# A trunk of attention, dense and expert layers: the first expert chosen on the chip, narrower first slot, whole weight chunks

## The chip, the cores and the metric

The kernel runs on one core of a Trainium2 chip, as one launch. The metric is the device time of an execution in microseconds (us). The engines of a core are TensorE (PE), VectorE (DVE), ScalarE (ACT), GpSimd (POOL) and SyncE (SP), each with its own instruction stream; they wait for each other by semaphores. DMAs are issued from SP, ACT and GpSimd queues.

## What is computed

512 tokens of width 1024 pass two post-norm layers. Layer 0 is sliding-window attention with cross-attention and a dense SwiGLU; layer 1 is forgetting attention with cross-attention and a top-2-of-8 mixture of experts. The part that matters here is the mixture (F is 2816):

```python
logits = (x2 @ w_router).astype(jnp.float32) + b_router.astype(jnp.float32)
top_vals, top_idx = lax.top_k(logits, TOP_K)
gates = jax.nn.softmax(top_vals, axis=-1)
...
def expert_block(args):
    xb, e = args
    h = xb @ w_in[e]
    return (jax.nn.silu(h[:, :D_FF]) * h[:, D_FF:]) @ w_out[e]
...
y = jnp.zeros_like(x2).at[slot_tok].add((ys * slot_gate[:, None]).astype(x2.dtype))
```

Each token goes to its two best experts, and a layer norm of 1.414 x + y follows. For the reference's inputs the experts 0 to 7 get 111, 128, 98, 133, 134, 128, 135 and 157 tokens; of the first 384 tokens 83, 95, 78, 108, 95, 95, 105 and 109.

## The kernel before

All weights are float32 and are read once, in chunks of 128 x 2048 (1 MiB). `Weights` (from L78) handles them: `load` issues a chunk's DMA on SP into a ring of raw buffers (7 in the expert part), `upper` writes the float16 high half `wh` on ACT (L149), and `lower` the float16 rest `wl` on DVE (L158), both in pieces of `PIECE` = 1048 columns (1048 and 1000). A ring of `NHL` = 7 chunks holds the halves. Each float32 product is three matmuls: wh by the high half of the activations, wh by their low half, wl by the high half (L1442 to L1444 and L1471 to L1473). `need` forces what a matmul needs; else the splitting advances by `tick`, which is called from within the products and issues one high piece and, one piece later, its low half. `tick` is called four times in a unit. Tile's scheduler keeps the order of each engine as the program is written, so where a `tick` stands sets what lies ahead of an instruction on ACT and DVE.

The expert part has eight slots, in a fixed order of work; slot s has `CAP[s]` places, that is columns of the activations, and the loops over it are unrolled. A table `TURN` says which rank by count sits in which slot, except that expert 0 is always in slot 0. Its token rows are gathered by matmuls with one-hots (`choose`, `oh_`), while the other slots' rows come by indirect DMA from the rows in HBM (`fetch`, `ready`). For slots 1 to 7 the expert's number is computed on DVE and read by SP (`value_load`, L296), and the chunk addresses come from it. Slot 0 has a fixed address, so its first chunks load ahead, during attention.

A slot has 22 input chunks (ten units of 512 columns in `block4`, two chunks and 96 matmuls each, and a `gate_pair`) and 11 output chunks (`down_wide`), 1584 matmuls in all; the last slot (`down_direct`) has 12 of them. Units come in pairs: even ones are the gate, odd ones the up half. A unit's products go to one of two PSUM banks (`bank2`). The gate's bank is read by ACT, the up half's by DVE (`quad`, L1458, tile `sa`: gate times up), after which ACT makes the high half of the product and GpSimd subtracts it (L1460). So unit i + 2 cannot start before unit i's bank is read, and for odd units that is an instruction in DVE's stream, behind all `wl` that stand ahead of it.

Between the units jobs are hung (`at`): in slot 6 the sums of the earlier slots come back from HBM (`token_sums`, unit 5), are normed (`stats`, units 7 and 8; `norm_out`, units 10 to 13), and the rows of slots 6 and 7 are joined to them in slot 7 (`rows_out`, `rows_done`). At the start, DVE also makes the list of slots (`order_of`, `lists`), the gates and their parts (`gates`, `gate_parts`), and one-hots (`places`).

## Time and profile before

| | us |
| --- | --- |
| median of 3 runs | 1633.73 |
| lowest to highest | 1633.63 to 1635.57 |
| the profiled execution | 1634.23 |
| its span, first to last instruction | 1632.4 |
| PE busy in the span | 1578.6 |
| DVE busy | 1210.9 |
| ACT busy | 950.3 |
| GpSimd busy | 267.7 |

The span holds attention and the dense layer up to about 789 us; the eight slots follow to 1620.5 us, and 12 us of last norms and stores. The profile's windows give the busy time of each engine in a stretch, and the granted clock of PE (1.00 is 2.4 GHz, 0.5 is 1.2 GHz). The timelines give each instruction's start and duration, and in brackets the idle time of its engine before it with what ended it.

### The profile page before, as it was taken

To read this page: it belongs to the slowest core of one execution; us is meant where nothing else is said; L and a number is where in the kernel's file an instruction comes from. 1 tells how busy PE (TensorE), PEld (TensorE's weight loads), DVE (VectorE), ACT (ScalarE), POOL (GpSimd) and SP (SyncE) were. 2 spreads that over 40 slices of the span, in tenths; PEclk is the share of its full clock that TensorE was granted. 3 is DMA by queue.
4 is the path that set the end of the run, shared out by engine and by line. 5 is a ranking of instruction groups with operands and counts; after the bars stand their busy time and mean duration, and the time that the engine had idled before them with its cause. 6 is when DMAs were issued, how large, how long until landed. Compare 5 with 4: busy or idle time off the path is not lost. (4 is left out here: it accounts for less than half of the span.)

```text
span 1632.4 us, 42978 instructions
## 1 busy us (share of the span) xinstructions
PE 1578.6 (97%) x18640; PEld 1267.8 (78%) x18640; DVE 1210.9 (74%) x1811; ACT 950.3 (58%) x1447; POOL 267.7 (16%) x264
## 2 busy tenths in 40 slices
...
GB/s 275 178 53 53 27 129 104 103 104 91 219 114 60 53 129 92 66 27 65 308 363 364 293 394 377 352 370 305 390 357 361 375 320 373 329 297 360 358 369 113
DMA packets 180549, 370.16 MB, mean 227 GB/s; under 512 B 6589, under 2 KB 49597, under 8 KB 180352
## 3 DMA queue, kind: packets, MB, share of 16 engines
...
q14 instruction: 49, 0.40, 0.1%
...
## 5 line engine op out<-in xcount | busy, mean ns | idle before, releaser
L158 DVE SCALAR_TENSOR_TENSOR wl<-raw,wh 128x1048 f16<-128x1048 f32 (+3 forms) x658 | 794.7, 1258 | 100.3 <-ACT wh L149 100.1
L149 ACT ACTIVATE wh<-raw 128x1048 f16<-128x1048 f32 (+3 forms) x658 | 641.8, 1036 | 101.7 <-PE bk L239 42.9
L1444 PE MATMUL bk<-xa,wl 128*128 128x160 f16 (+3 forms) x1280 | 260.0, 231 | 0.9 <-DVE wl L158 0.9
L1442 PE MATMUL bk<-xa,wh 128*128 128x160 f16 (+3 forms) x1280 | 260.1, 231 | 0.8 <-ACT xa L231 0.8
L1443 PE MATMUL bk<-xa,wh 128*128 128x160 f16 (+3 forms) x1280 | 260.0, 231 | 0.0
L1443 PEld LDWEIGHTS <-wh 128*128 128x128 f16 x2560 | 250.5, 98 | 3.6 <-issue 2.4
L1444 PEld LDWEIGHTS <-wl 128*128 128x128 f16 x2560 | 250.5, 98 | 1.3 <-DVE wl L158 1.1
L1442 PEld LDWEIGHTS <-wh 128*128 128x128 f16 x2560 | 250.4, 98 | 0.7
L1473 PE MATMUL bk<-act,wl 128*128 128x160 f16 (+6 forms) x1232 | 235.3, 227 | 1.2 <-DVE wl L158 1.2
L1472 PE MATMUL bk<-act,wh 128*128 128x160 f16 (+6 forms) x1232 | 235.3, 227 | 0.0
L1471 PE MATMUL bk<-act,wh 128*128 128x160 f16 (+6 forms) x1232 | 235.2, 227 | 0.0
L1442 PE MATMUL bk<-xe,wh 128*128 128x128 f16 (+2 forms) x1280 | 223.2, 221 | 2.2 <-DVE sa L1458 1.4
L1443 PE MATMUL bk<-xe,wh 128*128 128x128 f16 (+2 forms) x1280 | 223.1, 221 | 0.0
L1444 PE MATMUL bk<-xe,wl 128*128 128x128 f16 (+2 forms) x1280 | 223.1, 221 | 0.0
L237 PE MATMUL bk<-xTh,wh 128*128 128x512 f16 (+2 forms) x656 | 204.8, 322 | 1.2 <-DVE Kx L234 0.9
L239 PE MATMUL bk<-xTh,wl 128*128 128x512 f16 (+2 forms) x656 | 204.6, 322 | 1.4 <-DVE wl L158 1.4
L238 PE MATMUL bk<-xTl,wh 128*128 128x512 f16 (+2 forms) x656 | 204.6, 322 | 0.5 <-DVE xTl L234 0.5
L1460 POOL TENSOR_TENSOR act<-sa,act 128x512 f16<-128x512 f32 (+6 forms) x40 | 106.3, 2659 | 284.7 <-ACT act L231 284.6
L239 PEld LDWEIGHTS <-wl 128*128 128x128 f16 x944 | 92.4, 98 | 49.0 <-DVE wl L158 2.9
L237 PEld LDWEIGHTS <-wh 128*128 128x128 f16 x944 | 92.4, 98 | 48.7 <-ACT wh L149 2.0
L238 PEld LDWEIGHTS <-wh 128*128 128x128 f16 x944 | 92.5, 98 | 46.6 <-issue 1.5
L1473 PEld LDWEIGHTS <-wl 128*128 128x128 f16 x1232 | 120.5, 98 | 1.6 <-DVE wl L158 1.6
(349 smaller groups left out, 2669.2 us busy)
## 6 DMA issues: line engine op xcount, KB each, us to landing
...
```

The source lines that it names most:

```text
L149: self.nc.scalar.activation(h[:, p:e], t[:, p:e], AF.Copy, scale=SW)
L158: self.nc.vector.scalar_tensor_tensor(l, src, SW, h, op0=OP.mult, op1=OP.subtract)
L237: nc.tensor.matmul(o, lh, rh, start=first, stop=False, **kw)
L238: nc.tensor.matmul(o, lh, rl, start=False, stop=False, **kw)
L239: nc.tensor.matmul(o, ll, rh, start=False, stop=last, **kw)
L1442: nc.tensor.matmul(o, wh[:, k, c], xe[0][:, k, :C], start=first, stop=False, skip_group_check=True)
L1443: nc.tensor.matmul(o, wh[:, k, c], xe[1][:, k, :C], start=False, stop=False, skip_group_check=True)
L1444: nc.tensor.matmul(o, wl[:, k, c], xe[0][:, k, :C], start=False, stop=k == KD - 1, skip_group_check=True)
L1460: lambda: nc.gpsimd.tensor_sub(act[1][:, j, :C], sa[:, :, :C], act[0][:, j, :C])]
L1471: nc.tensor.matmul(o, wh[:, k, c], act[0][:, kk, :C], start=first, stop=False, skip_group_check=True)
L1472: nc.tensor.matmul(o, wh[:, k, c], act[1][:, kk, :C], start=False, stop=False, skip_group_check=True)
L1473: nc.tensor.matmul(o, wl[:, k, c], act[0][:, kk, :C], start=False, stop=kk == KF - 1, skip_group_check=True)
```

## The change

Slot 0 no longer holds expert 0. After three of four token tiles are routed, `fewest` counts those tokens on PE and takes, on DVE, the expert with the least; SP reads the number, and only then do slot 0's weights load (`W.shut` holds them back). Slot 0 has 128 places, so the third PSUM bank of the gathered rows goes away; the other slots' places and ranks change, 1154 places in all become 1126. In units 0 and 1 the two products with `wh` come first for both units and those with `wl` after. Four high pieces are forced before the rows of slot 0 are read from PSUM. Small chores (`gates_of`, `gate_parts`, `beyond`, one-hots) move behind the first splits. From the end of unit 1 on, chunks are split in one piece of 2048.

```diff
-CAP = [160, 128, 152, 134, 144, 140, 168, 128]
-TURN = [0, 6, 2, 5, 3, 4, 1, 7]
+CAP = [128, 168, 128, 154, 134, 146, 140, 128]
+TURN = [0, 1, 6, 2, 5, 3, 4, 7]
...
     def load(self):
         while self.dma < len(self.chunks):
             i = self.dma - self.from_
+            if i >= 0 and self.shut:
+                return
...
+    def need_high(self, i):
+        while self.hcut <= i:
+            assert self.upper(True)
+        return self.chunks[i][3][0]
...
-            expert[s] = nc.sync.value_load(eid[0:1, s:s + 1], min_val=0, max_val=NEXP - 1)
+            row = eid[0:1, s:s + 1] if s else e0i[0:1, 0:1]
+            expert[s] = nc.sync.value_load(row, min_val=0, max_val=NEXP - 1)
...
+    def fewest(pb):
+
+        for i in range(NT - 1):
+            nc.tensor.matmul(pb[:, 64:64 + NEXP], ones, selb[:, i, :], start=i == 0, stop=i == NT - 2)
+        key0 = small.tile([128, NEXP], FT, name="key0")
+        nc.vector.scalar_tensor_tensor(key0, pb[:, 64:64 + NEXP], float(NEXP), iota8, op0=OP.mult, op1=OP.add)
+        nc.vector.tensor_reduce(low0, key0, axis=AX.X, op=OP.min)
+        nc.vector.tensor_scalar(oh0, key0, low0, None, op0=OP.is_equal)
+        cross(key0, oh0, iota8, OP.mult)
+        nc.vector.tensor_reduce(low0, key0, axis=AX.X, op=OP.add)
+        nc.vector.tensor_copy(e0i, low0)
+        W.shut = False
+        W.load()
...
+    def first_list(t0, t1):
+
+        n = t1 - t0
+        own = small.tile([128, NT, NEXP], FT, name="own")[:, :n]
+        cross(own, posm[:, t0:t1], oh0[:, None, :].to_broadcast([128, n, NEXP]), OP.mult)
+        nc.vector.tensor_reduce(pos0[:, t0:t1], own, axis=AX.X, op=OP.add)
         for t in range(t0, t1):
-            nc.vector.tensor_scalar(oh_[0][:, t, :CAP[0]], iota_c[:, :CAP[0]], posm[:, t, 0:1], None, op0=OP.is_equal)
+            nc.vector.tensor_scalar(oh_[0][:, t, :CAP[0]], iota_c[:, :CAP[0]], pos0[:, t:t + 1], None, op0=OP.is_equal)
...
     finish(u_o1, mixT, gb1, out_left, turn1, aside)
+    first_list(0, NT - 1)
     turn1(NT - 1)
-    choose(range(6, 11), range(3))
+    choose(range(0, 8), range(3))
     pb = bank()
     route(NT - 1, pb)
-    choose(range(11, 2 * KD), range(3))
+    for _ in range(4):
+        W.upper(True)
+    choose(range(8, 2 * KD), range(3))
     ranks(NT - 1, NT, *rank_tmp())
     places_of(NT - 1, NT, pb)
+    first_list(NT - 1, NT)
...
-    def block4(C, u, xe, b, tick):
+    def block4(C, u, xe, b, tick, passes=(0, 1, 2)):
...
+                    for p in passes:
+                        if p < 2 and 2 not in passes:
+                            w = W.need_high(W.first[u] + kk // 4)[:, k % 4 * 512 + f * 128:k % 4 * 512 + f * 128 + 128]
+                        else:
+                            w = ws[p == 2][:, k, c]
...
     def order_of():
+        nc.vector.scalar_tensor_tensor(key, oh0, FAR * NEXP, first, op0=OP.mult, op1=OP.add)
+        nc.vector.scalar_tensor_tensor(key, pb[:, 64:64 + NEXP], float(NEXP), key, op0=OP.mult, op1=OP.add)
...
     def small_work():
-        lists()
-        yield
         gates()
         yield
+        yield
+        gates_of()
+        yield
         gate_parts()
+        yield
+        beyond()
         yield
...
-                b = bank2()
-                block4(C, u, XE[s], b, tick)
+                if (s, i) == (0, 0):
+                    ahead = [bank2(), bank2()]
+                    for v, b in zip(u_ei[s], ahead):
+                        block4(C, v, XE[s], b, lambda: None, (0, 1))
+                if s == 0 and i < 2:
+                    b = ahead[i]
+                    block4(C, u, XE[s], b, tick, (2,))
+                else:
+                    b = bank2()
+                    block4(C, u, XE[s], b, tick)
...
             if (s, i) == (0, 1):
-                _, _, *at_[0] = fetch(me, oh, blocks(0), False)
+                W.piece = CHUNK
```

Three places show what this makes of the engines' streams. The first is DVE ahead of the layer norm of token tile 3, in the changed kernel: `key`, `low`, `oh` and `e0i` are the new count and choice, `posm` and `xtok` the rows that stood there before.

```order
L432 BN_STATS st_8454<-xtok 128x6
L1231 SCALAR_TENSOR_TENSOR key_8618<-bk,iota_4523 128x8
L1232 TENSOR_REDUCE low_5853<-key_8618 128x1
L1233 TENSOR_SCALAR oh_5852<-key_8618,low_5853 128x8
L1170 TENSOR_TENSOR key_8618<-oh_5852,iota_4523 128x8
L1235 TENSOR_REDUCE low_5853<-key_8618 128x1
L1236 CAST e0i<-low_5853 128x1
L1170 TENSOR_TENSOR posm<-posm,bk 128x24
L431 SCALAR_TENSOR_TENSOR xtok<-xtok,bk 128x256
L432 BN_STATS st_8454<-xtok 128x6
L473 BN_AGGR mv<-st_8454 128x2
L438 TENSOR_SCALAR lnw<-mv 128x1
```

Six instructions stand ahead of `posm` and of the norm's `xtok` that stood together before. On SP, the load of `e0i` stands ahead of the first expert chunk, where the kernel before had 20 chunks of expert 0 in a row.

The second is DVE in slot 0 from the second `sa` (units 2 and 3) to the third (units 4 and 5), before:

```order
L1458 SCALAR_TENSOR_TENSOR sa<-bk_9368,sa 128x4x160
L158 SCALAR_TENSOR_TENSOR wl<-raw,wh 128x1000
...
L1357 CAST idx<-bk 128x1
L1370 SCALAR_TENSOR_TENSOR tow<-bk,spare 128x1
L1372 TENSOR_TENSOR to<-tow,bk 128x1
L158 SCALAR_TENSOR_TENSOR wl<-raw,wh 128x1000
L158 SCALAR_TENSOR_TENSOR wl<-raw,wh 128x1048
...
L158 SCALAR_TENSOR_TENSOR wl<-raw,wh 128x1048
L1458 SCALAR_TENSOR_TENSOR sa<-bk_9612,sa 128x4x160
```

and in the changed kernel:

```order
L1488 SCALAR_TENSOR_TENSOR sa<-bk_9297,sa 128x4x128
L161 SCALAR_TENSOR_TENSOR wl<-raw,wh 128x2048 x4
L1385 CAST idx<-bk 128x1
...
L1400 TENSOR_TENSOR to<-tow,bk 128x1
L1398 SCALAR_TENSOR_TENSOR tow<-bk,spare 40x1
...
L161 SCALAR_TENSOR_TENSOR wl<-raw,wh 128x2048 x4
L1710 TENSOR_REDUCE gown<-bk 128x1
L1488 SCALAR_TENSOR_TENSOR sa<-bk_9562,sa 128x4x128
```

Between these two `sa` stood eight pieces of `wl`, four chunks; now there are eight whole chunks. The lead of `wl` over the unit whose `sa` follows goes from four and a half chunks to six.

The third is DVE around the first `sa` of slot 7, whose units' rows `x` and `xg` are the joins of slot 6, before:

```order
L158 SCALAR_TENSOR_TENSOR wl<-raw,wh 128x1000
L1506 SCALAR_TENSOR_TENSOR x_20221<-bk,gown,x_20221 128x512
L1507 BN_STATS st_8947<-x_20221 128x6
L158 SCALAR_TENSOR_TENSOR wl<-raw,wh 128x1048
L1506 SCALAR_TENSOR_TENSOR xg_19598<-bk,gown,xg_19598 40x512
L1507 BN_STATS st_8947<-xg_19598 40x6
L158 SCALAR_TENSOR_TENSOR wl<-raw,wh 128x1000
...
L1507 BN_STATS st_8947<-xg_19598 40x6
L158 SCALAR_TENSOR_TENSOR wl<-raw,wh 128x1048
L158 SCALAR_TENSOR_TENSOR wl<-raw,wh 128x1000
L158 SCALAR_TENSOR_TENSOR wl<-raw,wh 128x1048
L1458 SCALAR_TENSOR_TENSOR sa<-bk_23141,sa 128x4x128
```

and in the changed kernel:

```order
L454 SCALAR_TENSOR_TENSOR xtok<-xtok,lnw_8892,lnb 128x512
L161 SCALAR_TENSOR_TENSOR wl<-raw,wh 128x2048 x6
L1536 SCALAR_TENSOR_TENSOR x_19811<-bk,gown,x_19811 128x512
L1537 BN_STATS st_8889<-x_19811 128x6
...
L1537 BN_STATS st_8889<-x_19811 128x6
L161 SCALAR_TENSOR_TENSOR wl<-raw,wh 128x2048
L1536 SCALAR_TENSOR_TENSOR xg_19208<-bk,gown,xg_19208 12x512
L1537 BN_STATS st_8889<-xg_19208 12x6
...
L1537 BN_STATS st_8889<-xg_19208 12x6
L161 SCALAR_TENSOR_TENSOR wl<-raw,wh 128x2048 x2
L1488 SCALAR_TENSOR_TENSOR sa<-bk_22635,sa 128x4x128
```

The joins stand between whole chunks now. The last norm pass of slot 6 stands two chunks later in the stream than before, and nine chunks of `wl` lie between it and this `sa`, as many as before.

## Rows read from the trace of the kernel before

**Rows 1.** The page, part 1.

```profile
PE 1578.6 (97%) x18640; PEld 1267.8 (78%) x18640; DVE 1210.9 (74%) x1811; ACT 950.3 (58%) x1447; POOL 267.7 (16%) x264
```

**Rows 2.** Windows, slots 0 to 2, 5, 6: length, then busy us by engine (instructions), PEclk, DMA, GB/s.

```profile
788.90:903.00 114.10, 112.36 (x1617) 111.50 (x1617) 98.82 (x130) 82.38 (x94) 16.27 (x6) 1.00 0.96 349
903.00:995.50 92.50, 92.50 (x1635) 92.09 (x1633) 85.38 (x89) 74.45 (x90) 25.78 (x9) 1.00 0.97 349
995.50:1102.90 107.40, 107.40 (x1627) 107.09 (x1625) 89.12 (x89) 74.68 (x90) 14.32 (x8) 1.00 1.01 363
...
1302.40:1402.90 100.50, 100.50 (x1636) 100.05 (x1634) 87.62 (x89) 77.32 (x94) 17.95 (x9) 1.00 0.99 354
1402.90:1522.10 119.20, 117.96 (x1619) 117.37 (x1617) 103.29 (x112) 75.89 (x88) 21.63 (x14) 1.00 0.97 322
```

**Rows 3.** Groups of lines by form, 788 to 1621 us: busy us, mean ns, idle before.

```profile
L158 DVE SCALAR_TENSOR_TENSOR wl<-raw,wh 128x1048 f16<-128x1048 f32 x262 | 354.8, 1354 | 67.0 <-ACT wh L149 66.9
L149 ACT ACTIVATE wh<-raw 128x1048 f16<-128x1048 f32 x262 | 279.8, 1068 | 38.3 <-PE bk L1472 19.0 <-DVE xtok L446 8.3 <-PE bk L1473 4.1
```

**Rows 4.** Windows, 20 us in the slot of 128 places (columns as in rows 2).

```profile
960.00:980.00 20.00, 20.00 (x362) 20.00 (x360) 20.00 (x20) 18.05 (x22) 5.93 (x1) 1.00 1.03 403
```

**Rows 5.** Timeline of DVE at the start of slot 0: start us, us, instruction.

```profile
788.14 1.29 DVE L1569 TENSOR_SCALAR xa<-bk 128x512 f16<-128x512 f32 x2 [0.52 <-PE bk L1241]
...
789.35 0.15 DVE L1561 COPY cnt<-bk 128x8 f32<-128x8 f32 x1
...
792.19 0.17 DVE L1599 TENSOR_SCALAR sel<-rank 128x32 f32<-128x32 f32 x1
...
797.28 0.42 DVE L1162 TENSOR_TENSOR g<-ose,gateE 128x256 f32<-128x256 f32 x1
...
799.41 4.62 DVE L158 SCALAR_TENSOR_TENSOR wl<-raw,wh 128x1000 f16<-128x1000 f32 x4
```

**Rows 6.** SP's DMAs and loads of numbers; moved GB/s, 770 to 800 us, 0.75 us each.

```profile
775.83 57.55 SPq L122 DMA_DIRECT2D raw<-in_w_exp_in_dram  x18
870.53 0.40 SPq L122 DMA_DIRECT2D raw<-in_w_exp_in_dram  x1
...
L296 SPq TENSOR_LOAD <-eid x7: 269/281/569, 868.5 to 1489.8; - x7
...
GB/s 0 0 0 0 0 0 0 22 0 85 197 380 410 410 404 393 390 391 380 336 276 415 412 407 418 382 391 412 404 401 396 399 401 401 385 391 360 60 38 16
```

**Rows 7.** Timeline of DVE, end of slot 6 and start of slot 7.

```profile
1513.59 0.75 DVE L446 SCALAR_TENSOR_TENSOR xtok<-xtok,lnw,lnb 128x512 f32<-128x512 f32 x1
...
1515.93 12.60 DVE L158 SCALAR_TENSOR_TENSOR wl<-raw,wh 128x1048 f16<-128x1048 f32 x11 [0.47 <-ACT wh L149]
1528.45 0.74 DVE L1506 SCALAR_TENSOR_TENSOR x<-bk,gown,x 128x512 f32<-128x512 f32 x1
1529.22 0.69 DVE L1507 BATCH_NORM_STATS2 st<-x 128x6 f32<-128x512 f32 x1
...
1540.76 0.68 DVE L1458 SCALAR_TENSOR_TENSOR sa<-bk,sa 128x512 f32<-128x512 f32 x1
```

**Rows 8.** Timeline of PE: three instructions that waited, idle before them and releaser.

```profile
779.86 1.84 PE L394 MATMUL bk<-identf,xtok 128*128 128x128 f32 x8 [2.46 <-DVE xtok L446]
...
1541.48 0.22 PE L1442 MATMUL bk<-xe,wh 128*128 128x128 f16 x1 [1.36 <-DVE sa L1458]
...
1605.66 0.27 PE L1518 MATMUL bk<-wl,act 128*128 128x256 f16 x1 [3.89 <-DVE wl L158]
```

**Rows 9.** Windows behind the first and the third of these (columns as in rows 2).

```profile
780.00:783.60 3.60, 3.60 (x41) 3.24 (x41) 1.85 (x3) 2.07 (x4) 2.31 (x2) 0.53 1.05 397
...
1606.20:1609.70 3.50, 3.31 (x18) 2.13 (x16) 3.46 (x5) 0.28 (x1) 3.50 (x1) 0.51 0.00 0
```

**Rows 10.** Timeline of GpSimd in slot 6: two subtractions.

```profile
1448.49 3.96 POOL L1460 TENSOR_TENSOR act<-sa,act 128x672 f16<-128x672 f32 x1
1463.72 1.55 POOL L1460 TENSOR_TENSOR act<-sa,act 128x672 f16<-128x672 f32 x1 [11.27 <-ACT act L231]
```

More of the change, by code (lines that the diff above doesn't have):

```diff
@@ L1171, in trunk_kernel @@
     selb = base.tile(V3, BF, name="selb")
+    oh0 = base.tile([128, NEXP], FT, name="oh0")
+    low0 = base.tile([128, 1], FT, name="low0")
+    e0i = base.tile([128, 1], I32, name="e0i")
+    pos0 = base.tile([128, NT], FT, name="pos0")
     pT = {}
@@ L1270, in aside @@
             oh_.append(op.tile([128, NT, CMAX], FH, name="PTh", bufs=2))
-            places_of(0, 3, bank())
+            pb3 = bank()
+            fewest(pb3)
+            places_of(0, 3, pb3)
         if (t, h, k) == (3, 1, 15):
-            xe_out.extend([bank2(), bank2(), bank()])
-            choose(range(0, 6), range(3))
+            xe_out.extend([bank2(), bank2()])
     def fox_all():
@@ L1431, in down_group @@
             tick()
[L1433 to L1435 removed]
+    def block4(C, u, xe, b, tick, passes=(0, 1, 2)):
+        ws = unit(u, 512)
         for kk in (0, 4):
@@ L1571, in trunk_kernel @@
     XE[0] = XA
-    chosen_to(XA, 0, range(3), lambda o, v: high(o, v, SX))
-    chosen_to(XA, 1, range(2), lower)
-    chosen_to(XA, 1, range(2, 3), lambda o, v: high(o, v, SX))
+    chosen_to(XA, 0, lambda o, v: high(o, v, SX))
+    chosen_to(XA, 1, lower)
     xTx.close()
@@ L1642, in trunk_kernel @@
     chores = small_work()
-    next(chores)
+    lists()
     pend = []
```

59 lines of the change are left out of this document (23 added, 36 removed).

## Prediction

> **What bounds the kernel now.** I read the page first, then windows with one stretch per slot, then lines and timelines of single engines. The page gives PE 97% of the span [rows 1]. The windows show why the span is what it is: from 788.9 us on, eight slots follow each other, and in slots 1 to 5 PE is busy for the whole stretch, 92.50 of 92.50 us in the slot of 128 places, 107.40 of 107.40 at 152 [rows 2]. A slot's time there is its matmul columns. The rows give the price of a place: (100.50 - 92.50)/12 = 0.67 us from 128 to 140, (107.40 - 92.50)/24 = 0.62 to 152; 1584 matmuls of a slot at one column per cycle of 2.4 GHz are 0.66 us, which I use. Second comes DVE: 85 to 103 us of a slot, of which the low halves (`wl`) are about 80: 33 pieces of 1048 at 1.35 us and 33 of 1000 at 1.2 [rows 2, 3]. In 960 to 980 it is busy for 20.00 of 20 us [rows 4], so it has nothing to give in the later part of a slot of 128 places, and lives on what it saved up in a wide one. DMA is not the limit: in the same 20 us it moves 403 GB/s, one chunk of 1.049 MB in 2.6 us, 33 chunks in 86, and no PE time is lost there.
>
> **The sum, in matmuls.** The places go from 1154 to 1126: 28 fewer, 28 x 0.66 = **-18.5 us** if PE stays as busy as now. By slot, before to after: slot 0 160 to 128 (-21.1), slots 1 to 5 698 to 730 (+21.1; row by row +19.5, since 152 and 168 cost less than 0.66 a place: slot 6 took 119.2, of which 1.2 was idle [rows 2]), slot 6 168 to 140 (118.0 to about 99.5, and the 1.2 us idle: -19.8), slot 7 unchanged. The routing of the reference's inputs sends 98 tokens to the expert chosen for slot 0, and no slot's count is over its places, so no further block runs. What matters is where those 41 us are taken away: from slot 0 and slot 6, the two slots in which DVE has extra work to do.
>
> **Start of slot 0.** Six small DVE instructions in a row, 0.15 to 0.23 us each as the neighbours of their kinds [rows 5], some 0.6 us ahead of layer norm of tile 3 once its own gaps take them up, so the norm's end at 780.5 and all behind it slip by that. Nothing of slot 0's weights can be asked for before the number is there (about 776.2). SP's load of a number costs 2.0 us from its start to the next DMA (868.5 to 870.53 [rows 6]), so chunk 0 is asked for at 778.3. From an issue at 775.83 the queue reached full rate 2.4 us later, and a chunk takes 2.7 us [rows 6]: it lands near 783, the next ones near 786, 789 and 793. Before, three chunks were loaded and split long before. The new order hides this: ACT's high halves of chunks 0 and 1 (1.07 us for 1048 columns [rows 3], 2.1 a chunk) fit between 783 and 788, and the high products of units 0 and 1, 2 x 64 matmuls of 55 ns, need no low half. PE should start at about 789.3 against 788.9. Unpriced is only the burst of loads beside the token rows; between 0 (chunk 0 before 785) and +3 us (a chunk later) I take 0.4.
>
> **DVE in slot 0.** From 788.6 it is behind and does not get free: `xa` 1.3, order and lists 2.9 and two more small ones 3.3, gates 1.3, gate_parts 2.2 [rows 5], gates_of 1.0 and beyond 0.8 (six and four of 0.17 to 0.2), one-hots and token numbers 3.3, three `sa` at 0.68 [rows 7], in all 15.3 us. The low halves up to chunk 17 come ahead of the third `sa` (as the order shows): eight in pieces and ten whole. Eleven pieces back to back took 12.60 us [rows 7], 2.29 us a chunk; their 11288 elements at one per 0.96 GHz cycle are 11.76, so a piece carries 0.077 us of its own and a whole chunk costs 2.21, an estimate. 8 x 2.31 + 10 x 2.21 = 40.6. A piece of 1048 that took 1.17 in such a row takes 1.354 in the mean of 262 [rows 3]; over 40 GpSimd subtractions in the program that is (0.184 x 262)/40 = 1.2 us for each. I put one in (the other of the two should fall beside small work), and the third `sa` is done at 788.6 + 15.3 + 40.6 + 1.2 = 845.7. Unit 7 needs the bank that it frees, and PE would be there at 838.8. So PE loses about 6.9 us, and with 912 of the 1584 matmuls still to come (53 us of the 92.5 in the slot of 128) slot 0 ends near 899 instead of 903: **-4** of its 21.1. Before, four chunks lay between unit and `sa`; now six, because whole chunks are cut at each of four ticks.
>
> A rule bears on the 0.077. The Trainium skill (VectorE: DVE Perf Modes, the section on the TRN2 errata) has a fixed cost per instruction, measured there near 150 cycles, against the 74 cycles of this row. By it, half the pieces would give 33 x 0.156 = 5.1 us a slot instead of 2.5; the row decides.
>
> **Slots 1 to 5.** DVE needs 85 to 88 us there [rows 2] and now about 2.5 less; PE needs 92.5 to 117. Covered: **+19.5**. In the one 128 slot (slot 2) the cover is the lead saved up in slot 1, which is 117 us wide.
>
> **Slots 6 and 7.** In slot 6 the token sums go to SBUF and four layer norms run on DVE (DVE 103.3 of 119.2, against 87.6 of 100.5 in slot 5 [rows 2]); before slot 7 its lead is gone: PE waited 1.36 us for the `sa` of slot 7's unit 1 [rows 8], done at 1541.44 [rows 7], while DVE had been busy since 1515.93 almost without a gap. With slot 6 shorter by 19.8 us PE arrives at unit 3 of slot 7 about 117 us after the start of slot 6. DVE has to do from the token sums (which land some 50 to 54 us in, the loads of weights waiting beside them) 21 or 22 whole chunks (47 to 49), statistics and norms 15 to 18 (0.75 us a pass [rows 7]), joins 5.7 (four of 0.74 and 0.69 [rows 7]), `sa` and `xe` 5: 73 to 78 us, and is there at 127 to 130. PE loses about 10 to 13. From unit 3 on the kernel before took 79 us (1541.5 to 1620.5), with the 3.89 us wait for a low half, 1.8 of slow clock behind it and shorter waits, some 7 in all [rows 8, 9]. DVE stands two whole chunks further ahead of PE at this `sa` than before (the order: chunk 240 instead of 238), 4.4 us, which takes most of these waits away. So 127 to 130 plus 72 to 73 against 217.6 before (1402.9 to 1620.5): slots 6 and 7 together give **-18.5 to -15**, I take -17; if the late waits stay, -11.
>
> **Clock.** After a PE idle of 2.46 us the granted clock was 0.53 for 3.6 us, after the wait of 3.89 us 0.51 for 3.5 us, the lower of the two levels; after 1.36 us it stayed at 1.00 [rows 8, 9]. Each of my two waits is longer, so each can cost half of 3.5 us. Where PE trickles with the low halves there may be no single long idle, so I count one of two: **+1.8**, with 0 and 3.5 as ends.
>
> Sum: 19.5 - 4 - 17 + 1.8 = +0.3 (the start's 0.4 is inside the -4), on the profiled run of 1634.23, which is 0.5 above the median of 1633.73. I forecast **1634 us** at the median: the change saves 18.5 us of matmuls and gets nearly all of it back as waits on DVE at two places. Measurement here tells about 0.2%, 3.3 us.
>
> **Rivals.**
> 1. *The whole chunks buy enough lead* (faster). If DVE's extra work lies in the deeper lead, since each tick may split a whole chunk and the ring has seven, the `sa` waits go. Then 1633.7 - 18.5, or 1615; half of it, 1624. For it: landed chunks were never late in slots 1 to 5, and DVE's mean load is 88%. Against: DVE 20.00 of 20 already [rows 4], and slot 0 starts with no lead. Chance 0.34 for over 3.3 us of gain.
> 2. *ACT and DVE take turns on whole chunks* (slower). Behind each break of DVE's work the next low half waits for a high half; now that is a whole piece of about 1.95 us [rows 3] instead of 1.05. Where DVE is late (about 10 breaks in slot 0, 8 around the norms) each break that waits costs up to 0.9 us: 18 x 0.9 = 16 at most, 8 likely: 1641; with the late waits of slot 7 kept, 1640 without it. It decides when DVE is later than 4.6 us (a unit of 5.3 less a `sa`) at an `sa`. Chance 0.28 for over 3.3 us of loss.
>    A second mechanism inside this case, 0.06 of the 0.28: GpSimd's `act` subtraction took 1.55 us by itself and 3.96 beside DVE's pieces [rows 10], and the second next `sa` waits for it. If its wait grows with the piece, by 1.03 us for each of the ten in slots 0 and 7, the sum is 1643. The Trainium skill (SBUF — State Buffer, Who interferes with whom) says this of the pair: a DVE instruction with two SBUF inputs and a GpSimd one that reads SBUF block each other, each for the whole of the other; the two rows agree in kind.
> 3. *DMA becomes the bound.* With slots of 128, 128 and 134 close together, 33 chunks want 92.5 us, 374 GB/s. The row reaches 403 [rows 4], so at most 0.02, at 1638; it is inside rival 2's range. The Trainium skill (DMA: Bandwidth & Descriptors, Bandwidth) gives about 358 GB/s for one core; by that a 128 slot would take 97 us, which the 92.50 [rows 2] rules out.
> 4. *The choice does nothing* (the same expert, as many places run): excluded by 128 columns in the program.
>
> **Numbers.** Forecast (within 0.2%) 0.38, faster 0.34, slower 0.28. My own case alone spans 1628 to 1640 (lateness of `sa` 2 us either way at each place, clock or not). The range that leaves out two in ten: **1622 to 1643**.
>
> **What would show it.** Right: PE idle of 5 to 8 us near 839 ended by DVE `sa`; slot 0 from 789.3 to about 899; clock at 0.5 behind it; slots 1 to 5 without waits, sum 519 us; a wait of about 10 us that begins near 1535 and is ended by `sa`; whole `wl` at 2.2 us. Wrong: slot 0 near 882, or no wait over 2 us in slot 7 (rival 1); ACT's `wh` named as releaser of DVE for over 8 us in these slots (rival 2); weights late on DMA at chunk 0.

## The result and the profile after

The changed kernel takes **1650.57 us** (median of four runs, 1649.29 to 1652.47) against 1633.68 of the kernel before: a ratio of 1.0102 with a 95% interval of 1.0084 to 1.0119. It is slower by 17 us, where 1634 was forecast and 1643 was the upper end. All interpretation below is of the profiled executions, 1650.6 us of span against 1632.4.

The page's part 1 of the changed kernel, to be held beside [rows 1]:

```profile
PE 1573.1 (95%) x18563; PEld 1261.5 (76%) x18563; DVE 1185.9 (72%) x1561; ACT 929.5 (56%) x1186; POOL 261.2 (16%) x263
```

PE and DVE both have less to do than before (PE 5.5 us less, DVE 25.0 less), and the span is 18.2 us longer. The loss is waiting, and slow clock that counts as busy time. The windows of slots 0, 1, 2, 5, 6 and 7, with the columns of [rows 2]:

```profile
790.90:901.50 110.60, 98.44 (x1625) 96.69 (x1625) 104.45 (x117) 83.79 (x68) 14.46 (x7) 0.92 1.03 381
901.50:1018.30 116.80, 116.80 (x1612) 116.77 (x1610) 83.27 (x51) 73.14 (x53) 18.51 (x7) 1.00 0.93 326
1018.30:1110.80 92.50, 92.50 (x1635) 92.11 (x1633) 82.46 (x57) 72.09 (x57) 19.31 (x9) 1.00 1.02 364
...
1316.00:1420.40 104.40, 104.40 (x1636) 103.92 (x1634) 85.76 (x57) 75.12 (x59) 19.94 (x9) 1.00 0.99 354
1420.40:1535.80 115.40, 103.86 (x1619) 102.81 (x1617) 94.18 (x78) 65.87 (x52) 27.52 (x14) 0.96 0.93 314
1535.80:1638.70 102.90, 95.39 (x1273) 84.91 (x1270) 93.15 (x77) 71.69 (x59) 27.37 (x10) 0.93 0.82 289
```

Slots 1 to 5 are full, as forecast: PE is busy 116.80 of 116.80 and 92.50 of 92.50 us at clock 1.00. All that PE loses behind its start is in slot 0 (PE busy 98.4 of 110.6, clock 0.92), slot 6 (103.9 of 115.4, 0.96) and slot 7 (95.4 of 102.9, 0.93). PE's timeline names the waits, in brackets:

```profile
780.71 1.97 PE L402 MATMUL bk<-identf,xtok 128*128 128x128 f32 x8 [4.08 <-DVE xtok L454]
...
805.86 1.67 PE L1474 MATMUL bk<-xa,wl 128*128 128x128 f16 x14 [2.95 <-DVE wl L161]
...
846.24 0.39 PE L1474 MATMUL bk<-xa,wh 128*128 128x128 f16 x2 [5.84 <-DVE sa L1488]
...
1481.71 0.39 PE L1474 MATMUL bk<-xa,wh 128*128 128x140 f16 x2 [5.79 <-DVE sa L1488]
...
1521.74 0.23 PE L1503 MATMUL bk<-act,wl 128*128 128x140 f16 x1 [2.03 <-DVE wl L161]
...
1529.24 0.23 PE L1501 MATMUL bk<-act,wh 128*128 128x140 f16 x1 [1.61 <-ACT wh L152]
...
1531.57 0.30 PE L1503 MATMUL bk<-act,wl 128*128 128x140 f16 x1 [2.03 <-DVE wl L161]
...
1541.40 0.28 PE L1474 MATMUL bk<-xe,wl 128*128 128x128 f16 x1 [2.04 <-DVE wl L161]
...
1546.55 1.11 PE L1522 MATMUL bk<-identf,yt 128*128 128x128 f32 x4 [2.64 <-ACT yt L1515]
...
1565.09 0.27 PE L1474 MATMUL bk<-xe,wh 128*128 128x128 f16 x2 [2.07 <-DVE sa L1488]
```

The row at 805.86 is the longest of several waits for the first low halves of slot 0 (0.83, 1.14 and 2.95 us, and shorter ones). Two long ones end with DVE's `sa`, 5.84 us in slot 0 and 5.79 in slot 6; then come several of about 2 us, four of them ended by one half of a chunk, one by ACT's `yt` and the last by the first `sa` of slot 7. Windows of the stretches behind them:

```profile
804.20:814.40 10.20, 7.63 (x69) 7.10 (x70) 10.03 (x16) 10.19 (x11) 0.00 (x0) 0.50 1.03 367
845.10:851.90 6.80, 5.66 (x54) 5.66 (x55) 6.50 (x8) 5.14 (x5) 2.47 (x1) 0.50 1.06 384
1480.00:1486.80 6.80, 5.09 (x45) 5.09 (x45) 6.43 (x6) 5.11 (x6) 2.53 (x1) 0.50 1.05 297
1541.40:1551.70 10.30, 7.66 (x62) 7.26 (x63) 10.30 (x5) 10.30 (x11) 0.00 (x0) 0.50 0.89 299
```

In these four stretches, 34.1 us in all (two shorter ones, at 1531 and 1565, aside), the granted clock is 0.50, the lower level; before, the whole expert part had one such stretch, of 3.5 us [rows 9].

I took the same sums from the trace of each run's profiled execution: the first matmul of slot 0, the length of slot 0, of slots 1 to 5, of 6 and of 7, and in those the idle time of PE (from one matmul's start to the next, beyond the usual distance) and what matmuls lost at the lower clock, in us. The last column is the median of all runs of that kernel.

| run | start | slot 0 | 1 to 5 | slot 6 | slot 7 | idle | slow clock | median |
| --- | --- | --- | --- | --- | --- | --- | --- | --- |
| before | 788.9 | 114.1 | 499.9 | 119.2 | 98.3 | 11.1 | 2.1 | 1633.7 |
| **changed** | 790.9 | 110.6 | 519.0 | 115.4 | 102.8 | 34.1 | 15.4 | 1650.6 |
| pieces kept | 789.2 | 107.4 | 521.8 | 122.0 | 103.6 | 51.1 | 5.6 | 1659.0 |
| slot 6 wide | 789.8 | 110.5 | 500.7 | 117.7 | 100.9 | 23.0 | 8.5 | 1633.4 |
| before, whole chunks | 788.9 | 119.0 | 499.9 | 117.7 | 101.1 | 14.1 | 5.0 | 1640.2 |
| before, slot 6 narrow | 789.1 | 114.1 | 518.4 | 113.5 | 97.4 | 19.5 | 5.7 | 1647.3 |
| expert 0 fixed | 790.1 | 103.8 | 519.3 | 115.6 | 101.0 | 29.6 | 11.1 | 1643.6 |
| statistics two units later | 791.8 | 110.7 | 519.3 | 99.2 | 112.2 | 34.0 | 9.3 | 1647.2 |
| stores on SP | 790.6 | 109.6 | 519.0 | 107.2 | 100.0 | 29.7 | 7.6 | 1640.7 |
| stores on SP, statistics one later | 791.8 | 109.6 | 519.0 | 99.2 | 104.4 | 27.7 | 5.8 | 1637.6 |
| before, stores on SP | 786.1 | 114.0 | 499.9 | 117.7 | 96.9 | 8.1 | 2.1 | 1632.0 |
| slot 6 wide, stores on SP | 789.8 | 110.5 | 500.7 | 117.7 | 91.2 | 15.4 | 6.0 | 1623.9 |
| the same, high products not first | 787.8 | 111.1 | 500.7 | 117.7 | 91.2 | 15.4 | 6.3 | 1623.2 |
| the same, pieces kept | 791.6 | 108.0 | 502.4 | 130.0 | 104.1 | 39.8 | 6.3 | 1648.1 |
| the same, short lead in slot 0 | 789.3 | 105.2 | 501.8 | 117.7 | 91.2 | 13.2 | 3.2 | **1619.2** |
| and expert 0 fixed | 789.3 | 94.5 | 503.5 | 117.7 | 91.2 | 7.8 | 0.0 | **1611.0** |

Before to changed, the span's +18.2 is: 2.0 at the start, +23.0 of idle, +13.3 of slow clock, and a remainder of -20.1 for the matmuls. The change's arithmetic came in as forecast; it was given back almost twice. The start alone varies from run to run: the nine runs that share the changed kernel's code up to slot 0 begin it between 789.2 and 791.8 us, the four that share the kernel before's between 786.1 and 789.1. The kernel before was timed again with each group of runs, at 1633.7 to 1635.3 us, so medians of different groups compare to about 1.5 us.

### The profile page after: what moved, and what is told of

The parts are those of the page before. It is cut to its first block, busy times and chain, and to the rows that moved or that the text cites. A ratio compares the mean times of both kernels' runs of the same rounds, so it can differ in the third digit from the quotient of the medians.

```text
span 1650.6 us, 42422 instructions
## 1 busy us (share of the span) xinstructions
PE 1573.1 (95%) x18563; PEld 1261.5 (76%) x18563; DVE 1185.9 (72%) x1561; ACT 929.5 (56%) x1186; POOL 261.2 (16%) x263
## 5 line engine op out<-in xcount | busy, mean ns | idle before, releaser
L161 DVE SCALAR_TENSOR_TENSOR wl<-raw,wh 128x2048 f16<-128x2048 f32 (+4 forms) x401 | 761.2, 1925 | 139.4 <-ACT wh L152 135.1
L152 ACT ACTIVATE wh<-raw 128x2048 f16<-128x2048 f32 (+4 forms) x401 | 623.3, 1580 | 189.5 <-PE bk L247 40.8
L1474 PEld LDWEIGHTS <-wh 128*128 128x128 f16 x5120 | 412.2, 99 | 16.5 <-issue 9.0
L1474 PE MATMUL bk<-xe,wh 128*128 128x168 f16 (+3 forms) x2560 | 255.1, 230 | 2.5 <-DVE sa L1488 2.1
L1474 PE MATMUL bk<-xe,wl 128*128 128x168 f16 (+3 forms) x1280 | 252.9, 230 | 2.0 <-DVE wl L161 2.0
L1474 PE MATMUL bk<-xa,wh 128*128 128x128 f16 (+2 forms) x2560 | 228.6, 224 | 12.4 <-DVE sa L1488 11.6
L1503 PE MATMUL bk<-act,wl 128*128 128x128 f16 (+5 forms) x1232 | 230.4, 226 | 4.1 <-DVE wl L161 4.1
L1501 PE MATMUL bk<-act,wh 128*128 128x128 f16 (+5 forms) x1232 | 230.5, 226 | 1.7 <-ACT wh L152 1.6
L1474 PE MATMUL bk<-xa,wl 128*128 128x128 f16 (+2 forms) x1280 | 225.0, 226 | 6.3 <-DVE wl L161 6.3
L1502 PE MATMUL bk<-act,wh 128*128 128x128 f16 (+5 forms) x1232 | 230.4, 226 | 0.0
L1490 POOL TENSOR_TENSOR act<-sa,act 128x512 f16<-128x512 f32 (+5 forms) x40 | 103.9, 2597 | 300.5 <-ACT act L239 300.3
L245 PEld LDWEIGHTS <-wh 128*128 128x128 f16 x944 | 92.4, 98 | 49.0 <-ACT wh L152 2.3
L246 PEld LDWEIGHTS <-wh 128*128 128x128 f16 x944 | 92.4, 98 | 46.7 <-issue 1.5
L1501 PEld LDWEIGHTS <-wh 128*128 128x128 f16 x1232 | 121.0, 98 | 2.0 <-ACT wh L152 2.0
L1502 PEld LDWEIGHTS <-wh 128*128 128x128 f16 x1232 | 121.0, 98 | 0.0
```

The costliest lines, as they stand in the source:

```text
L152: self.nc.scalar.activation(h[:, p:e], t[:, p:e], AF.Copy, scale=SW)
L161: self.nc.vector.scalar_tensor_tensor(l, src, SW, h, op0=OP.mult, op1=OP.subtract)
L245: nc.tensor.matmul(o, lh, rh, start=first, stop=False, **kw)
L246: nc.tensor.matmul(o, lh, rl, start=False, stop=False, **kw)
L1474: nc.tensor.matmul(o, w, xe[p == 1][:, k, :C], start=p == 0 and k == 0 and f % 2 == 0, stop=p == 2 and k == KD - 1, skip_group_check=True)
L1490: lambda: nc.gpsimd.tensor_sub(act[1][:, j, :C], sa[:, :, :C], act[0][:, j, :C])]
```

## The experiments

Two theories stood against each other after the result. W: whole chunks make ACT and DVE take turns around the norms. N: slot 6 of 140 places leaves DVE too little time, whatever the pieces.

**Pieces kept**, whole chunks undone:

```diff
             if (s, i) == (0, 1):
-                W.piece = CHUNK
+                W.piece = PIECE
```

> The changed kernel with its weights split in pieces of 1048 and 1000 throughout (the one line that sets whole chunks undone). Theory W: whole chunks fill the ring of seven in program order, so that no high half is written ahead when a norm pass comes, and ACT and DVE take turns there (DVE waits 2.44 us at each of three norm passes where the kernel before waited 0.47). Then the late waits of slots 6 and 7 (7.7 us after 1521 and the slow clock behind them) shrink by most: 1633 to 1640 us against 1650.6. Theory N (slot 6 of 140 places instead of 168 leaves DVE too little time, whatever the pieces): 1647 us or more, with PE waits of over 15 us in slots 6 and 7.

1659.0 us (ratio to before 1.0149, 1.0131 to 1.0166): slower still, by 8 us, which is theory N's range. Whole chunks helped this kernel. The run does not settle theory W, though, for it undoes more than the size of a piece. I count, in DVE's stream at each `sa` of units 0 to 9, the columns of `wl` that stand ahead of it beyond what the units up to this one need, in chunks of 2048: a lead of 3.5 at all of them in the kernel before (not four and a half, as said with the change), of 1.0, 2.0 and then 6.0 nearly throughout in the changed kernel, and with pieces kept of 1.0 in slot 0 and 1.5 after it. With whole chunks undone, the changed kernel has less than half the lead of the kernel before.

**Slot 6 wide**, the slots of 168 and 140 places exchanged, and **the kernel before with slot 6 narrow**:

```diff
-CAP = [128, 168, 128, 154, 134, 146, 140, 128]
-TURN = [0, 1, 6, 2, 5, 3, 4, 7]
+CAP = [128, 140, 128, 154, 134, 146, 168, 128]
+TURN = [0, 4, 6, 2, 5, 3, 1, 7]
```

```diff
-CAP = [160, 128, 152, 134, 144, 140, 168, 128]
-TURN = [0, 6, 2, 5, 3, 4, 1, 7]
+CAP = [160, 128, 152, 134, 144, 168, 140, 128]
+TURN = [0, 6, 2, 5, 3, 1, 4, 7]
```

> The changed kernel with the slots of 168 and 140 places exchanged (168 in slot 6, 140 in slot 1), whole chunks kept; the sum of places stays. Theory N: slot 6 gets 18 us of PE time back in front of the norms and its waits go: 1631 to 1637 us. Theory W: DVE still needs 9.8 us for two chunks and a norm pass, against 7.0 of PE, the waits stay in part: 1642 to 1650 us. Both: slot 1 of 140 places without waits.

> The kernel before with the slots of 168 and 140 places exchanged (140 in slot 6, 168 in slot 5), pieces kept. Theory N: slot 6 loses 18 us of PE time in front of the norms, and waits of 10 us or more with slow clock come in slots 6 and 7: 1643 to 1650 us. Theory W: pieces keep a high half ahead, waits grow by 5 us at most: 1634 to 1638 us.

1633.4 us (0.9991, 0.9981 to 1.0000), and 1647.3 (1.0073, 1.0048 to 1.0097). The sum of places is the same in each pair; only its order differs. The order alone is worth 17 us in the changed kernel and 12 in the kernel before. Theory N holds from both sides. Slots 6 and 7 of the wide run, by the columns of [rows 2]:

```profile
1401.00:1518.60 117.60, 117.60 (x1618) 117.44 (x1616) 92.73 (x79) 67.81 (x52) 25.64 (x14) 1.00 0.93 309
1518.60:1619.60 101.00, 92.31 (x1273) 81.95 (x1270) 92.74 (x76) 71.23 (x59) 27.42 (x10) 0.97 0.84 296
```

Slot 6 is without a gap (117.60 of 117.60) and slot 7 still loses 8.7 us and some clock.

**The kernel before with whole chunks**: one line, `W.piece = CHUNK` behind unit 1 of slot 0.

> The kernel before with whole chunks from the end of unit 1 on, and nothing else of the change. Theory W: DVE waits 2.4 instead of 0.5 us for ACT at each norm pass of slot 6, and PE loses that there and the slow clock behind it: 1640 to 1648 us against 1633.7. Theory N: whole chunks save 0.077 us a piece and hurt nowhere in a slot 6 of 168 places: 1629 to 1634 us.

1640.2 us (1.0034, 1.0022 to 1.0047). Slower, at the lower end of W's range, though mostly not for its reason: slot 0 lost 4.9 us (PE waited 3.36 at 829 for an `sa` that stands behind more chunks), and slots 6 and 7, where the norms are, lost 1.3 together (slot 7 lost 2.8, slot 6 gained 1.5). Whether the lead of 6.0 instead of 3.5 paid for the turns there was not tried apart.

**Expert 0 fixed in slot 0**, so that its chunks load during attention (the count is multiplied by 0; the first four forced pieces are asked for and not forced):

```diff
-    expert = {}
+    expert = {0: 0}
...
-        self.shut = True
+        self.shut = False
...
-        nc.vector.scalar_tensor_tensor(key0, pb[:, 64:64 + NEXP], float(NEXP), iota8, op0=OP.mult, op1=OP.add)
+        nc.vector.scalar_tensor_tensor(key0, pb[:, 64:64 + NEXP], 0.0, iota8, op0=OP.mult, op1=OP.add)
...
-        W.upper(True)
+        W.upper(False)
```

> The changed kernel with expert 0 always in slot 0 (its counting and choosing instructions still run, with a factor of 0 on the counts), so that its first chunks load and split during attention as in the kernel before; 128 places, high products first and whole chunks stay. Theory L: what slot 0 loses (13.5 us of waits and 6.0 of slow clock) comes from the three chunks whose low halves (6.9 us of DVE) now fall after 788 us, and from nothing being split when PE arrives: slot 0 shrinks from 110.6 to about 97 to 101 us and the time to 1637 to 1641. Rival C: the chores of DVE against a slot of 128 places are the cause, and slot 0 stays above 106 us, the time above 1645.

1643.6 us (1.0056, 1.0039 to 1.0073); slot 0 103.8, between the two. The load behind the choice cost 6.8 us of slot 0, about the three low halves (3 x 2.28). The rest had another cause, which the short lead below finds.

**Statistics two units later**, and with them inverse and norms:

```diff
-        at(L6, 7 if t < 2 else 8, lambda t=t: stats(t))
-        at(L6, 10 + t, lambda t=t: norm_out(t, gbx))
-    at(L6, 9, lambda: inverse(lnw, mvs[:, :, 1], 1.0))
+        at(L6, 9 if t < 2 else 10, lambda t=t: stats(t))
+        at(L6, 12 + t, lambda t=t: norm_out(t, gbx))
+    at(L6, 11, lambda: inverse(lnw, mvs[:, :, 1], 1.0))
```

> The changed kernel with the statistics, the inverse and the four norm passes of slot 6 two units later each (statistics at units 9 and 10 instead of 7 and 8). Theory T: the 6.07 us wait at 1482 is DVE standing in front of statistics whose token sums have not landed, with the sa of unit 7 behind it; it goes, with the slow clock behind it: 1640 to 1645 us. Rival D: DVE's work in slot 6 is too much for 140 places anyway, and the same time comes back as waits around the norms and in slot 7: 1648 to 1654 us.

1647.2 us (1.0078, 1.0061 to 1.0094): slot 6 took 99.2 us without any wait, which is what the forecast had for it, and slot 7 112.2, with one wait of 16.22:

```profile
1543.81 1.12 PE L1522 MATMUL bk<-identf,yt 128*128 128x128 f32 x4 [16.22 <-ACT yt L1515]
```

The time lies between the two ranges, and both were half right: the statistics are what held slot 6, and the work came back in slot 7. How the statistics held it is seen in the changed kernel, GpSimd's requests first and then DVE:

```profile
1456.10 3.08 POOL L1387 DMA_INDIRECT xg<-x_rows,idx  x1 [2.49 <-DVE to L1400]
...
1464.12 4.10 POOL L1733 DMA_DIRECT2D xtok<-expert_sums  x4
```

```profile
1475.63 1.29 DVE L1741 BATCH_NORM_STATS2 st<-xtok 128x6 f32<-128x512 f32 x2 [2.58 <-DMA xtok<-expert_sums]
...
1479.51 1.29 DVE L1741 BATCH_NORM_STATS2 st<-xtok 128x6 f32<-128x512 f32 x2 [2.35 <-DMA xtok<-expert_sums]
...
1480.96 0.69 DVE L1488 SCALAR_TENSOR_TENSOR sa<-bk,sa 128x560 f32<-128x560 f32 x1
```

The token sums are asked for at 1464.12 to 1465.83, and DVE stands 2.58 and 2.35 us before its statistics until the first two land, 11.5 and 14.8 us after their requests. The `sa` of unit 7 stands behind. The kernel before asked 42.8 us into its slot 6 and this one 43.7 (1464.1 - 1420.4), though its six units there are 6.7 us shorter: the request stands in GpSimd's stream behind three gathers, the first of which waited for DVE's `to` until 1456.10, and does not hang on PE. PE had stood in front of unit 9 for 5.79 us by then.

**Stores on SP**: the four norm passes send their rows out from SP instead of ACT.

```diff
     def norm_out(t, gb):
         centred(xtok[:, t, :], mvs[:, t, 0:1], lnw[:, 3, t:t + 1], gb, 128)
-        nc.scalar.dma_start(out[0, t * 128:(t + 1) * 128, :], xtok[:, t, :])
+        nc.sync.dma_start(out[0, t * 128:(t + 1) * 128, :], xtok[:, t, :])
```

> The changed kernel with the stores of the four norm passes issued on SP instead of ACT. Theory A: ACT stands 6.1 us before each of these stores until DVE's norm is done, so the next high half starts only then and DVE waits 2.4 us for it; with the stores on SP DVE's waits at the norm passes fall under 0.5 us, and PE's waits after 1521 (2.25, 1.84, 2.26, 2.26, 2.95) mostly go: 1638 to 1643 us. Rival R: the ring of seven is full, so the high half could not be written earlier in any case: 1648 to 1652 us.

> The run with 168 places in slot 6 (1633.4 us) with the stores of the norm passes on SP. Theory A: its waits at the start of slot 7 (9.6 us, 2.6 of slow clock) shrink by half or more: 1623 to 1629 us, which is faster than the kernel before. Rival R: 1631 to 1635 us.

> The kernel before with the four stores of the norm passes issued on SP and nothing else. Theory A: ACT stands 4.1 us before each store there too, with pieces that cost DVE only 0.47 us a pass; PE's small waits from 1507 to 1558 (4.3 us in all) go and some of the late one at 1605: 1627 to 1631 us. Rival: the stores cost the kernel before nothing, 1632 to 1635 us, and the whole of what the store gave the changed kernel was made by whole chunks.

1640.7 us (1.0039, 1.0025 to 1.0053), 9.9 less than the changed kernel; with slot 6 wide 1623.9 (0.9937, 0.9920 to 0.9953); the kernel before 1632.0 (0.9987, 0.9977 to 0.9997), 2 less, at the lower end of the rival's range there, though its interval leaves out that the stores cost nothing. In the changed kernel theory A holds. With 168 places in slot 6 in both, moving the stores gave 9.5 us with whole chunks and 2.1 with pieces, so most of what the stores cost seems to go with whole chunks; the two kernels differ in other things too. Against the changed kernel, the wide slot 6 gave 17.2 us, the stores 9.9 and both together 26.7: the two causes add up, and W's turns are the second of them. In the changed kernel ACT, then DVE, around one norm pass:

```profile
1516.99 0.35 ACTq L1746 DMA_DIRECT2D out_dram<-xtok  x1
1517.44 3.71 ACT L152 ACTIVATE wh<-raw 128x2048 f16<-128x2048 f32 x2 [6.55 <-DVE xtok L454]
```

```profile
1516.21 0.75 DVE L454 SCALAR_TENSOR_TENSOR xtok<-xtok,lnw,lnb 128x512 f32<-128x512 f32 x1
1519.39 4.49 DVE L161 SCALAR_TENSOR_TENSOR wl<-raw,wh 128x2048 f16<-128x2048 f32 x2 [2.43 <-ACT wh L152]
...
1539.05 11.10 DVE L161 SCALAR_TENSOR_TENSOR wl<-raw,wh 128x2048 f16<-128x2048 f32 x5 [2.44 <-ACT wh L152]
```

ACT has stood 6.55 us before a store that needs DVE's norm, writes the next high half only then, and DVE stands 2.43 us for it; in the kernel before the same gap was 0.47 [rows 7]. With the stores on SP the next DVE instruction follows on the norm without a bracket:

```profile
1511.42 0.75 DVE L454 SCALAR_TENSOR_TENSOR xtok<-xtok,lnw,lnb 128x512 f32<-128x512 f32 x1
1512.09 4.49 DVE L161 SCALAR_TENSOR_TENSOR wl<-raw,wh 128x2048 f16<-128x2048 f32 x2
1516.49 0.75 DVE L450 SCALAR_TENSOR_TENSOR xtok<-xtok,mvs,lng 128x512 f32<-128x512 f32 x1
```

**Stores on SP, statistics one unit later**, with 140 places in slot 6 (the edits of the last two, with 8, 9, 10 and 11 for the units):

> The changed kernel with the stores on SP (1640.7 us, 140 places in slot 6) and statistics, inverse and norm passes one unit later. Theory T: the 6.3 us wait at 1481 is token sums that land some 11 us after they are asked for, with sa behind the statistics; a unit (5.9 us) later they have landed, and with ACT free the norms do not bring it back: 1632 to 1636 us. Rival D: the wait comes back in slot 7, as when both the stores stayed on ACT and the statistics were two units late: 1639 to 1644 us.

1637.6 us (1.0019, 1.0009 to 1.0028), 3 less than with the stores alone and between the two expectations. Slot 6 is free of waits again, and one of 9.99 us for an `sa` stands at 1550 in slot 7:

```profile
1550.20 0.37 PE L1474 MATMUL bk<-xe,wh 128*128 128x128 f16 x2 [9.99 <-DVE sa L1488]
```

From 1476.5 to the end of that `sa` DVE is busy 71.58 of 73.64 us (the third busy time of the row):

```profile
1476.50:1550.14 73.64, 61.62 (x1014) 60.76 (x1012) 71.58 (x68) 47.48 (x39) 11.79 (x4) 0.96 1.04 370
```

So with 140 places it is not the late landing alone; DVE's work in slots 6 and 7 did not fit in any of the three places tried for the norms, and here almost no idle time of DVE is left to explain the wait.

**Short lead in slot 0**, on the run with slot 6 wide and stores on SP:

```diff
-        W.tick(1 if W.hcut >= W.done + LEAD else 2)
+        if W.piece == PIECE:
+            W.tick(1 if W.hcut >= W.done + LEAD else 2)
+        elif W.hcut < W.done + LEAD + 1 or W.cut - W.from_ > 20:
+            W.tick(1)
```

> The run with 168 places in slot 6 and stores on SP (1623.9 us), with whole chunks split at most five ahead of the last freed one until 21 chunks of slot 0 are done, so that the third sa of slot 0 stands behind four chunks instead of eight since the second. Theory S: the 6.0 us wait at 845 and the 3.4 us of slow clock behind it come from the chunks that stand ahead of that sa; they go: 1615 to 1619 us. Rival D: DVE's whole work in slot 0 is the limit, the wait comes back as waits for low halves: 1621 to 1626 us.

1619.2 us (0.9911, 0.9895 to 0.9928). The third `sa` of slot 0, at 845.50 in the changed kernel, stands at 834.52 here:

```profile
836.62 8.90 DVE L161 SCALAR_TENSOR_TENSOR wl<-raw,wh 128x2048 f16<-128x2048 f32 x4
...
845.50 0.68 DVE L1488 SCALAR_TENSOR_TENSOR sa<-bk,sa 128x512 f32<-128x512 f32 x1
```

```profile
829.24 4.49 DVE L161 SCALAR_TENSOR_TENSOR wl<-raw,wh 128x2048 f16<-128x2048 f32 x2
...
834.52 0.68 DVE L1488 SCALAR_TENSOR_TENSOR sa<-bk,sa 128x512 f32<-128x512 f32 x1
```

The wait at 846 is gone and slot 0 is 5.3 us shorter than on the same base with the long lead. Theory S holds, with 0.2 us less gained than the least that it expected. The lead of `wl` at the first four `sa` is 1.0 chunk here, where it was 1.0, 2.0, 6.0 and 6.0.

**High products not first**, the three products of a block in a row in units 0 and 1 too, on the same base without the short lead (`ahead` and the two passes removed, `block4` called as for the other units):

> The run with 168 places in slot 6 and stores on SP (1623.9 us), with the high products of units 0 and 1 not first: each weight block has its three products in a row, as elsewhere. Theory L: DVE sets the pace of slot 0 until its third sa at 845, so it does not matter in which order PE waits: 1622 to 1626 us, with PE idle near 791 to 797 in place of 800 to 806. Rival H: the order saves what it hides, some 6 us: 1629 to 1633 us.

1623.2 us (0.9937, 0.9920 to 0.9954) against 1623.9 with them: no difference. PE waits 4.70 us until 792.8 instead of later, and DVE's work decides when slot 0 goes on. This part of the change did nothing by itself; whether it helps once DVE is lighter was not tried.

**Pieces kept**, on the same base:

> The run with 168 places in slot 6 and stores on SP (1623.9 us), with pieces of 1048 and 1000 throughout. Theory P: once slot 6 is wide and ACT free, whole chunks give only 2.5 us of DVE a slot, which PE does not see, and pieces put the third sa of slot 0 earlier (slot 0 took 107.4 us with pieces, 110.5 with whole chunks): 1618 to 1622 us. Rival G: the deeper lead of whole chunks is what carries slots 6 and 7, as their removal cost 8.4 us with 140 places: 1626 to 1634 us.

1648.1 us (1.0081, 1.0064 to 1.0098): 24 us lost, more than either theory had. In slot 6 DVE now stands 7.14 us in front of the `sa` of unit 1, with four low halves behind it; at that place in the kernel before low halves were done first and the same `sa` followed without idle time:

```profile
1417.91 0.86 DVE L1488 SCALAR_TENSOR_TENSOR sa<-bk,sa 128x672 f32<-128x672 f32 x1 [7.14 <-PE bk L1474]
1418.68 5.89 DVE L161 SCALAR_TENSOR_TENSOR wl<-raw,wh 128x1000 f16<-128x1000 f32 x4
```

```profile
1418.48 1.25 DVE L158 SCALAR_TENSOR_TENSOR wl<-raw,wh 128x1048 f16<-128x1048 f32 x1 [0.38 <-ACT wh L149]
1419.64 0.85 DVE L1458 SCALAR_TENSOR_TENSOR sa<-bk,sa 128x672 f32<-128x672 f32 x1
```

Then ACT stands 6.98 us for weights; four chunks asked for from 1442.6 to 1455.0, around the requests of the token sums and before those landed, took 16.3 to 19.9 us to land, against 5 to 7 for those of the 20 us before:

```profile
1467.95 1.08 ACT L152 ACTIVATE wh<-raw 128x1048 f16<-128x1048 f32 x1 [6.98 <-DMA raw<-in_w_exp_in_dram]
```

The order of halves and `sa` is the lead counted above: 1.5 chunks at this `sa` here, 3.5 in the kernel before. So what whole chunks give this kernel seems to be lead, and not their 0.077 us a piece. That its lead with pieces is lower than the kernel before's because nothing is split when slot 0 begins was not tried apart.

**And expert 0 fixed**, on the short lead:

> The run with 168 places in slot 6, stores on SP and the short lead in slot 0 (1619.2 us), with expert 0 fixed in slot 0, so that its first three chunks load and split during attention. Theory L: what slot 0 still loses (10.4 us of waits, 3.2 of slow clock) is the load behind the choice and the three low halves after 788 us; slot 0 falls from 105.2 to 95 to 99 us and the time to 1609 to 1613. Rival C: DVE's chores and the order of its work are the rest, slot 0 stays above 102 us, the time above 1616.

1611.0 us (0.9856, 0.9839 to 0.9872), the fastest of all: 23.6 us faster than the kernel before in the same runs. Slot 0, short lead with and without the choice on the chip:

```profile
789.30:883.80 94.50, 91.72 (x1624) 90.76 (x1624) 91.41 (x110) 77.13 (x63) 19.99 (x7) 1.00 1.00 365
```

```profile
789.30:894.50 105.20, 96.81 (x1624) 93.85 (x1624) 100.87 (x116) 79.79 (x65) 13.54 (x7) 0.95 1.02 369
```

91.7 of 94.5 us busy at clock 1.00, against 96.8 of 105.2 at 0.95. Theory L holds: what was left of slot 0's loss was the load behind the choice. With 128 places this form needs an expert 0 of at most 128 tokens to stay without a further block, as the kernel before needed one of 160.

## Why the prediction was wrong

- **The sum in matmuls** was right: -18.5 forecast, or -20.1 by the prediction's own figures for each slot, -20.1 measured as the remainder, and slots 1 to 5 without waits, 519.0 us for 519.4.
- **Start of slot 0**: 789.3 forecast, 790.9 measured, within the 789.2 to 791.8 of the same code. PE's wait for the norm of tile 3 grew from 2.46 [rows 8] to 4.08 us with the clock behind it. Chunk 0 was asked for at 777.1 (778.3 forecast), and its high half began at 783.4 without a wait for it (783 forecast).
- **DVE in slot 0** was right in mechanism and place, and in size with some luck: the third `sa` was done at 846.18 for 845.7, PE's wait 5.84 for 6.9. DVE's `xa` began 1.6 us later than the 788.6 of the sum, and the work behind it was about as much shorter. The 838.8 at which PE was to come has no working; 672 matmuls at the rate of the slot of 128 places, from 789.3 on, would give 828.5. The waits and the slow clock from 800 to 814 that fill the difference had no price. Whole chunks in a row take 2.22 us (five in 11.10, the last row of DVE around the norms), 2.21 was estimated from 0.077 us a piece. By an estimate from the fixed cost near 150 cycles, 0.156 us, that the Trainium skill has (VectorE: DVE Perf Modes, the section on the TRN2 errata), it would have been 2.13. The trace does not agree with that, by its 2.22. Slot 0 was to end at 899 and ended at 901.5, by the slow clock.
- **Slots 6 and 7** is the step that failed: "I take -17", and together they took 218.2 us against 217.5, +0.7. The sum gave DVE 73 to 78 us of work from the token sums to the first `sa` of slot 7, nothing for standing idle, and had it there 127 to 130 us after the start of slot 6 (50 to 54 plus 73 to 78 would be 123 to 132). The work was right: 75.21 us from the first landing to the end of that `sa` (the third busy time of the row).

```profile
1475.63:1565.04 89.41, 70.77 (x1027) 68.85 (x1026) 75.21 (x70) 49.54 (x41) 8.51 (x4) 0.89 0.89 309
```

But DVE is idle for 14.2 of these 89.4 us, the first sums land at 55.2 us, and it is there at 144.6. First, the statistics stand in DVE's stream inside slot 6 with an `sa` behind them, and token sums landed no earlier though PE was faster; so PE lost 5.79 us in slot 6, which was to run its 99.5 without a wait. Second, the turns of ACT and DVE stood only in rival 2, at up to 0.9 us a break; three of them cost 2.0 each more than before. What follows that `sa` was right: 73.6 us to the end of slot 7 (72 to 73 forecast), and the late wait of 3.89 us [rows 8] was gone. The wait of about 10 us that was to show it came to 2.07 (at 1565.09), since PE had lost the time before. With both oversights taken out, in the run with stores on SP and statistics one unit later, this step comes out as forecast: DVE is there after 129.7 us, PE waits 9.99, and slots 6 and 7 take 203.6 us (199 to 203 forecast).
- **Clock** is the term that was mis-sized most: +1.8 with 3.5 as upper end, measured +13.3, which the lengths of the slots above contain. I priced one stretch of 3.5 us for a wait. The trace has six of 3.4 to 10.3 us besides the start's; they stand behind long waits and rows of short ones.
- **Rival 2** named the right side, and its turns are real: stores on SP gave 9.9 us. Its price of 8 us was near that by luck, since it came from 18 breaks of up to 0.9, halved, and the norms have three breaks of 2.4; the time it gave, 1641 (1642 by its own terms), was 10 short, for it had neither slot 6's wait nor the clock. Its sign says little: ACT's `wh` ends 20.3 us of DVE's idle time in slots 0, 6 and 7, but 28.1 in the kernel before. **Rival 1** was right that the deeper lead counts, as the leads of the two runs with pieces suggest. It was not enough in slot 6 with 140 places, where the faster time came only with 168 and the stores on SP.

The Trainium skill (SBUF — State Buffer, Who interferes with whom), named beside rival 2, has a DVE instruction with two SBUF inputs contend with a GpSimd instruction that reads SBUF, for ports that they share. A low half on DVE (`raw` and `wh`) and the subtraction on GpSimd are such a pair. The rows of the subtraction's line, min, median and max in ns, in the changed kernel and in the run with pieces kept:

```profile
L1490 POOL TENSOR_TENSOR act<-sa,act x40: 1729/2518/4494, 815.5 to 1606.9; 128x512 f16<-128x512 f32 x15, 128x672 f16<-128x672 f32 x5, 128x616 f16<-128x616 f32 x5, 128x536 f16<-128x536 f32 x5
```

```profile
L1490 POOL TENSOR_TENSOR act<-sa,act x40: 1252/1548/4874, 813.8 to 1606.6; 128x512 f16<-128x512 f32 x15, 128x672 f16<-128x672 f32 x5, 128x616 f16<-128x616 f32 x5, 128x536 f16<-128x536 f32 x5
```

2.52 us in the median beside whole chunks and 1.55 beside pieces: the trace agrees in kind. The 1.55 us that the prediction read as the subtraction by itself [rows 10] stand beside low halves too (DVE runs two from 1462.76 to 1466.38); beside none, it took 1.25 at 1481.1 in the run with pieces kept. No run shows that it reached PE. The price named there, ten waits of 1.03 us, would have made 1644 and not 1643.
